# An encoder layer in float32: the output norm's reciprocal roots brought to all partitions by DMA in place of matmuls, and made two steps earlier

## The chip, the cores and the metric

The kernel runs on one core of one Trainium2 chip. The metric is the device time of one execution in microseconds; lower is better. A core has five engines that work side by side, each on its own queue of instructions: PE (TensorE, matmuls; its weight loads are listed as PEld), DVE (VectorE), ACT (ScalarE), POOL (GpSimd) and SP (SyncE, which here issues nearly all DMA transfers). Each engine takes its instructions strictly in order, and an instruction that waits holds up all that stand behind it on the same engine. SBUF is the memory on the core, with 128 partitions; PSUM holds what PE writes, in eight banks; DRAM is reached by DMA.

## The reference

One layer of an encoder, applied with the same weights to a prompt of 2048 tokens and a sample of 512, each with 16 learned meta tokens ahead:

```python
def mixer_layer(h, norm_g, w_in, na_rpb, sink, w_proj_a, w_proj_b, w_out, t5_bias):
    u = rms_norm(h, norm_g)
    proj = u @ w_in                                   # 1024 x 5376
    qa, ka, va, za, qb, kb, vb, zb, ga, gb = jnp.split(proj, cuts, axis=-1)
    o_a = neighbourhood_attention(qa, ka, va, na_rpb) # 8 heads, 8 x 16 window of a 64-wide grid
    o_b = window_attention(qb, kb, vb, t5_bias, sink) # 8 query heads, 2 key heads, +-128 tokens
    y_a = (o_a * silu(za)) @ w_proj_a
    y_b = (o_b * silu(zb)) @ w_proj_b
    merged = sigmoid(ga) * y_a + sigmoid(gb) * y_b
    return merged @ w_out

h = h + mixer_layer(h, ...)
y = rms_norm(h[:, N_META:], final_g)                  # x * rsqrt(mean(x * x) + 1e-6) * g
```

All data is float32. The change touches both norms: the one at the input, for two of the five windows of tokens, and the one at the output, for four of the five.

## The kernel before, in words

Everything is kept with features on the partitions and tokens along the free axis. The 2560 tokens are five windows of 512: window 0 is the sample, 1 to 4 are the prompt. A float32 product is made of three matmuls of a high and a low part (`mm3`); the low part of a weight tile is a subtraction, on DVE or, in the later stages, on POOL (`wt`, line 190).

*The input projection* comes first, in two passes over the weights, each for two windows (`pairs`, with the products of line 762), and stages in which window 4 is projected alone. `prep_ahead(2)` runs as a generator between the products of the first pass. It sums the squares of windows 2 and 3 on POOL, sums them over the partitions with 8 matmuls against a column of ones (`fin_v`, line 468), makes the reciprocal roots on DVE (`rsqrt`, lines 142 to 152, three Newton steps), and so holds them as a 128 x 8 tile: token c * 128 + p on partition p, column c. What it needs is a row with all 512 values on every partition. For that `diagonal` (line 166, DVE) puts each column on the diagonal of a 128 x 128 block, `spread` (line 174, PE) multiplies the blocks with ones into a PSUM bank, and ACT copies the bank to SBUF (`rsa`, line 486). DVE then scales the inputs by it (line 359).

*Attention and the dense stages* follow. The loop at the end of the program takes attention units of 128 queries, and between them pulls steps from a generator `dense` of the window before: `dense_pb`, `dense_out` (the projection `w_out`), and `dense_pa` of the window itself. A step is half an output tile of `dense_pa` (six matmuls) and the like. `dense_out` leaves its result in `hT` (8 tiles), and POOL adds the squares to `ssq` (line 1245). `dense_fin(w - 1)` is the output norm: four matmuls sum `ssq` over the partitions (`sums`, line 159), then `rsqrt`, `diagonal`, five steps later `spread` and ACT's copy to `rbs` (line 1255), and then in each step POOL multiplies one `hT` by `rbs` (line 1259) and SP stores it (`out_dram`). `with_fill` interleaves it with `dense_pa`: after each step of `dense_pa` one of `dense_fin`. It runs four times, for windows 0 to 3; window 4's norm is made elsewhere (`finish_end`) and is not touched.

PSUM in this part: two banks `s` for scores, three `tp` for transpositions of the softmax, one `o`, and two `d` for the dense products. In the first part: five `mm` and three `vt`.

The order on PE is the order of the program's text. The orders on DVE, ACT, POOL and SP are made by a scheduler from the text and a model of times. A DMA that SP issues waits on SP for what it reads and for the buffer it fills. DMAs use eight completion counters in turn, and one also waits for the DMA that had its counter before. SP's line is 131 (`move`) for all.

Of the kernel before, what the change touches and what calls it, by code (L numbers as in the profile page):

```python
# [9 lines left out]
F32 = mybir.dt.float32  # L10
# [7 lines left out]
P = 128  # L18
# [7 lines left out]
WTOK = 512  # L26
NWIN = TOK // WTOK
# [60 lines left out]
def encoder_block(ctx: ExitStack, tc: tile.TileContext, xT, x_end, w_in, w_pa, w_pb, w_o, norm_g, final_g,  # L88
                  final_row, bias_a0, bias_a1, bias_a2, bias_a3, bias_b, bias_b0, outT_p, outT_s, out_e):
    nc = tc.nc  # L90
# [4 lines left out]
    def dt(name, shape):  # L95
        return dram.tile(shape, F32, tag=name, name=name)
# [9 lines left out]
    vb_d = dt("vb", [TOK, 2, P])  # L106
    vbm_d = dt("vbm", [N_META, 2, P])
    z_d = {(b, w, p): dt(f"z{b}{w}{p}", [P, WTOK]) for b in "ab" for w in range(NWIN) for p in range(4)}
    pre_d = dt("pre", [P, 4, 7, WTOK])
    wo_d = [dt(f"wo{c}", [P, 2, KT, WTOK]) for c in range(2)]  # L110
    g_d = {(b, w, f): dt(f"g{b}{w}{f}", [P, WTOK]) for b in "ab" for w in range(NWIN) for f in range(KT)}
# [27 lines left out]
    def rsqrt(small, sq, m, nc_):  # L139

        ve, hv, r, t = (small.tile([P, 8], F32, tag=f"rs{i}", name=f"rs{i}")[:m, :nc_] for i in range(4))
        nc.vector.tensor_scalar(ve, sq, 1.0 / D_MODEL, EPS, ALU.mult, ALU.add)
        nc.vector.tensor_scalar(r.bitcast(I32), ve.bitcast(I32), 1, None, ALU.arith_shift_right)
        nc.vector.tensor_scalar(r.bitcast(I32), r.bitcast(I32), -1.0, float(0x5F3759DF), ALU.mult, ALU.add)
        nc.vector.tensor_scalar(hv, ve, -0.5, None, ALU.mult)
        for _ in range(3):
            if nc_ == 1:
                nc.vector.scalar_tensor_tensor(t, r, hv, r, ALU.mult, ALU.mult)
            else:
                nc.vector.tensor_mul(t, r, hv)  # L150
                nc.vector.tensor_mul(t, t, r)
            nc.vector.scalar_tensor_tensor(r, t, 1.5, r, ALU.add, ALU.mult)
        return r
# [9 lines left out]
    def diagonal(dg, r, m):  # L163

        nc_ = r.shape[1]
        nc.vector.tensor_mul(dg[:m, : nc_ * m].rearrange("p (c n) -> p c n", n=m),
                             ident[:m, None, :m].broadcast_to([m, nc_, m]),
                             r[:m, :, None].broadcast_to([m, nc_, m]))

    def spread(psum, tag, dg, m, nc_):  # L170

        rb = psum.tile([P, WTOK], F32, tag=tag, name="rs_rb")
        for c in range(nc_):
            nc.tensor.matmul(rb[:, c * P : c * P + m], ones[:m, :], dg[:m, c * m : c * m + m], start=True, stop=True)
        return rb

    wpool = ctx.enter_context(tc.tile_pool(name="wpool", bufs=2))
    lo_eng, low = [nc.vector], [None]
# [269 lines left out]
    def prep_ahead(w):  # L448


        x0 = st.tile([P, 4, WTOK], F32, tag="x0", name="xa", bufs=1)
        x = x0[:, 2:4]
        for n in range(KT):
            k, i = n // 2 * 2, n % 2
            move(x, xT[k * P : (k + 2) * P, (w + i) * WTOK : (w + i + 1) * WTOK].rearrange("(k p) t -> p k t", p=P))
            yield
            acc = x0[:, i]
            nc.scalar.activation(x, x, AF.Square)
            if n < 2:
                nc.gpsimd.tensor_add(acc, x[:, 0, :], x[:, 1, :])  # L460
            else:
                for j in range(2):
                    nc.gpsimd.tensor_add(acc, acc, x[:, j, :])
            yield
        v = ps_t.tile([P, WTOK], F32, tag="vt", name="fin_v")
        for i in range(2):
            for c in range(4):
                nc.tensor.matmul(v[:, 4 * i + c : 4 * i + c + 1], x0[:, i, c * P : (c + 1) * P], ones[:, 0:1],
                                 start=True, stop=True)
        r = rsqrt(uxp, v[:, :8], P, 8)  # L470
        dgs = [ev.tile([P, WTOK], F32, tag="t", name="rs_dg", bufs=3) for _ in range(2)]
        for i in range(2):
            diagonal(dgs[i], r[:, 4 * i : 4 * i + 4], P)
        yield
        for kk in range(4):
            x0 = st.tile([P, 4, WTOK], F32, tag="x0", name="xa", bufs=1)
            for half in range(2):
                move(x0[:, 2 * half : 2 * half + 2],
                     xT[(kk + 4 * half) * P : (kk + 4 * half + 1) * P, w * WTOK : (w + 2) * WTOK]
                     .rearrange("p (i t) -> p i t", t=WTOK))  # L480
            yield
            if kk == 0:
                rss = []
                for i in range(2):
                    rss.append(ev.tile([P, WTOK], F32, tag="t", name=f"rsa{i}", bufs=3))
                    nc.scalar.copy(rss[i], spread(ps_t, "vt", dgs[i], P, 4))
            x = [x0[:, j] for j in range(4)]
            tt = ev.tile([P, 2, WTOK], F32, tag="ev", name="tt")
            for j in range(4):
                scale(x[j], kk, j, rss)  # L490
            nc.vector.tensor_sub(tt[:, 0], x[b22], x[b12])
            nc.vector.tensor_sub(x[b12], x[b12], x[b11])
            nc.vector.tensor_sub(tt[:, 1], x[b22], x[b12])
            t4 = ev.tile([P, 2, WTOK], F32, tag="ev", name="t4")[:, 0]
            nc.vector.tensor_sub(t4, x[b21], tt[:, 1])
            yield
            move(pre_d[:, kk, 0:4], x0)
            move(pre_d[:, kk, 4:6], tt)
            move(pre_d[:, kk, 6], t4)
            yield  # L500
# [669 lines left out]
    pools = {}  # L1170
# [74 lines left out]
                nc.gpsimd.tensor_add(ssq, ssq, x)  # L1245

    def dense_fin(w):
        r = rsqrt(pools["d"], sums(acc["s", w], 0, P, 4, ps_d, "d"), P, 4)
        dg = pools["d"].tile([P, WTOK], F32, tag="rbs", name="rs_dg", bufs=1)
        diagonal(dg, r, P)  # L1250
        for _ in range(5):
            yield
        rb = spread(ps_d, "d", dg, P, 4)
        rbs = pools["d"].tile([P, WTOK], F32, tag="rbs", name="rbs", bufs=1)
        nc.scalar.copy(rbs, rb)
        for f in range(KT):
            hT = acc["h", w, f]
            with tc.issue_after(low[0]):
                nc.gpsimd.tensor_mul(hT, hT, rbs)
            dst = outT_s if w == 0 else outT_p  # L1260
            c0 = 0 if w == 0 else (w - 1) * WTOK
            move(dst[f * P : (f + 1) * P, c0 : c0 + WTOK], hT)
            yield
# [92 lines left out]
    def phases(w, br):  # L1356

        if br == "a":
            if w == 0:
                yield from islice(gates, GATES_A)  # L1360
            else:
                yield from dense_pb(w - 1)
                yield from dense_out(w - 1, range(0, 4))
        elif w == 0:
            yield from gates
            open_dense()
            yield from dense_pa(0)
        else:
            yield from dense_out(w - 1, range(4, 8))
            pa = dense_pa(w)  # L1370
            yield from islice(pa, 3)
            yield from with_fill(pa, dense_fin(w - 1))


# [190 lines left out]
```

## Time and profile before

| what | value |
|---|---|
| median of 3 runs | 1909.06 us (1908.71 to 1910.85) |
| the profiled execution's own time | 1908.84 us |
| its span, first to last instruction | 1906.5 us |
| TensorE clock granted | 0.998 of full speed |
| matmuls `rs_rb` (line 174) in the span | 74 records, first at 31.8 us, last at 1821.6 us |
| multiplications of `hT` on POOL (line 1259) | 32, from 1317.3 us to 1833.6 us |
| DMA | 423.78 MB, q1 busy 66.8% of 16 engines' span |

Times in the profile are microseconds from the span's start. A row of a timeline is: start, length, engine, line, operation, what it writes and reads, shape, count; in brackets the idle time just ahead and what ended it. A row of the waits is: engine, line, what was waited for, total, times, longest. A row of the windows is: the stretch, then busy time and number of instructions of PE, PEld, DVE, ACT and POOL, the granted clock, the DMA share and GB/s. A float32 matmul leaves two records. The span holds four stretches that matter here, one for each `dense_fin`, which begin at about 1299, 1470, 1641 and 1809 us, and one of the first pass, at about 296 to 330 us.

### The profile page before, as it was taken

How to read it: one execution, taken by the hardware profiler on the slowest of the kernel's cores; microseconds unless marked ns; L12 is line 12 of the kernel's file. 1: busy time of each engine (PE TensorE's matmuls, PEld its weight loads, DVE VectorE, ACT ScalarE, POOL GpSimd, SP SyncE). 2: the span in 40 equal slices, each digit the busy share in tenths (PEclk: the TensorE clock that was granted, in tenths of full speed). 3: DMA queues.
4: the chain of work that ended last, by engine and by line, in shares of the span. 5: the costliest groups of instructions: out<-in, count | busy, mean ns of one | idle time of the engine just before them, and what ended most of it. 6: DMA issues, size and time to landing. Idle time of an engine off the chain costs nothing.

```text
span 1906.5 us, 29720 instructions
## 1 busy us (share of the span) xinstructions
PE 1878.5 (99%) x9925; PEld 1599.4 (84%) x9925; DVE 1320.3 (69%) x2887; ACT 1147.6 (60%) x2515; POOL 731.9 (38%) x556
## 2 busy tenths in 40 slices
PE   8999999999999999999999999999999999999998
PEld 6998888888888888888878888888888888888886
DVE  8886455556477544445457788878987887888874
ACT  6454443434464444444356787797788788878932
POOL 2005342323103232323223335655844773585420
PEclk9999999999999999999999999999999999999999
DMA  7667554645296765644368877977986996697473
GB/s 261 218 190 293 175 198 165 218 174 177 83 353 218 239 210 194 194 138 160 105 207 289 254 217 261 294 223 242 319 270 185 307 316 217 197 326 252 124 289 141
DMA packets 223760, 423.78 MB, mean 222 GB/s; under 512 B 49640, under 2 KB 90808, under 8 KB 222072
## 3 DMA queue, kind: packets, MB, share of 16 engines
q1 hardware_dynamic: 223320, 421.88, 66.8%
q8 instruction: 79, 1.29, 0.3%
q14 instruction: 73, 0.60, 0.1%
q10 hardware_dynamic: 288, 0.01, 0.0%
HBM read 303.07 MB, written 118.74 MB: 221 GB/s over the span
## 4 chain that ended last, share of the span: by engine, by line
PE 75%; DVE 9%; ACT 6%; DMA 5%; issue 3%; POOL 2%; SPq 0%; ACTq 0%; DVEq 0%; POOLq 0%
PE pa L762 21%; PE pe L762 10%; PE pc L762 5%; PE mm L135 4%; PE mm L137 4%; PE mm L136 4%; PE tp L1027 2%; PE pso L137 2%; PE pso L135 2%; PE pso L136 2%; PE tp L1129 1%; PE oa L1044 1%; PE oa L1042 1%; DVE s L953 1%; DMA wo<-wos 1%
## 5 line engine op out<-in xcount | busy, mean ns | idle before, releaser
L190 POOL TENSOR_TENSOR wt<-wraw,wt 128x512 fp32r<-128x512 f32 x164 | 215.4, 1331 | 288.2 <-ACT wt L189 288.1
L762 PE MATMUL pa<-u,wt 128*128 128x512 f32 x1008 | 242.9, 390 | 0.0
L762 PE MATMUL pa<-u,x 128*128 128x512 f32 x984 | 237.8, 390 | 0.0
L189 ACT CAST wt<-wraw 128x512 fp32r<-128x512 f32 x312 | 177.9, 620 | 73.8 <-PE mm L137 37.6
L762 PEld LDWEIGHTS pa<-u,wt 128*128 128x128 f32 x1008 | 188.7, 188 | 39.0
L762 PEld LDWEIGHTS pa<-u,x 128*128 128x128 f32 x984 | 183.9, 188 | 38.1
L733 POOL TENSOR_TENSOR s<-wraw,raw 128x512 f32<-128x512 f32 x40 | 57.9, 1447 | 271.7 <-DVE x L190 271.7
L135 PE MATMUL mm<-u,wt 128*128 128x512 f32 (+2 forms) x416 | 151.6, 364 | 7.3 <-ACT u L316 7.3
L728 POOL TENSOR_TENSOR s<-raw 128x512 f32<-128x512 f32 x40 | 60.0, 1500 | 253.3 <-DMA raw<-in_w_in_dram 137.0
L136 PE MATMUL mm<-u,wt 128*128 128x512 f32 (+2 forms) x416 | 147.5, 355 | 1.5 <-DVE u L317 1.5
L137 PE MATMUL mm<-u,wt 128*128 128x512 f32 (+2 forms) x416 | 147.5, 355 | 0.8 <-DVE wt L190 0.8
L190 DVE TENSOR_TENSOR wt<-wraw,wt 128x512 fp32r<-128x512 f32 x148 | 104.6, 746 | 61.6 <-ACT wt L189 61.5
L762 PE MATMUL pe<-u,wt 128*128 128x512 f32 x504 | 121.9, 391 | 0.0
L762 PE MATMUL pc<-u,wt 128*128 128x512 f32 x504 | 121.1, 389 | 0.0
L1031 DVE TENSOR_TENSOR pl<-tp,ph 128x512 fp32r<-128x512 f32 (+7 forms) x160 | 98.8, 617 | 24.0 <-ACT ph L1030 22.3
L762 PE MATMUL pe<-u,x 128*128 128x512 f32 x480 | 115.3, 389 | 0.0
L960 ACT ACTIVATE pr<-s,nm 128x384 f32<-128x384 f32 (+5 forms) x160 | 91.3, 571 | 37.9 <-DVE nm L953 35.4
L762 PEld LDWEIGHTS pc<-u,wt 128*128 128x128 f32 x504 | 94.6, 188 | 19.6
L762 PEld LDWEIGHTS pe<-u,wt 128*128 128x128 f32 x504 | 94.2, 188 | 19.4
L741 POOL TENSOR_TENSOR s<-wraw,s 128x512 f32<-128x512 f32 x40 | 52.9, 1322 | 146.2 <-DVE wt L190 146.2
L1030 ACT CAST ph<-tp 128x512 fp32r<-128x512 f32 (+7 forms) x160 | 84.7, 529 | 38.7 <-PE tp L1027 36.5
L135 PE MATMUL pso<-mh,wt 128*128 128x512 f32 x256 | 107.1, 418 | 0.0
(238 smaller groups left out, 5050.7 us busy)
## 6 DMA issues: line engine op xcount, KB each, us to landing
wraw<-in_w_in_dram SPq DMA_DIRECT2D x86, 512.0 KB
qa<-evq SPq DMA_DIRECT2D x20, 1024.0 KB
raw<-in_w_in_dram SPq DMA_DIRECT2D x40, 512.0 KB
q<-qa SPq DMA_DIRECT2D x20, 1024.0 KB
wraw<-in_w_o_dram SPq DMA_DIRECT2D x32, 512.0 KB
kbt<-kb SPq DMA_DIRECT2D x32, 384.0 KB
qb<-evq SPq DMA_DIRECT2D x20, 512.0 KB
ka<-evk SPq DMA_DIRECT2D x20, 512.0 KB
```

What stands on the lines that cost most here:

```text
L135: nc.tensor.matmul(ps, wh, uh, start=first, stop=False)
L136: nc.tensor.matmul(ps, wh, ul, start=False, stop=False)
L137: nc.tensor.matmul(ps, wl, uh, start=False, stop=last)
L189: nc.scalar.copy(h, r)
L190: low[0] = (eng or lo_eng[0]).tensor_sub(l, r, f32(h)).ins
L728: eng.tensor_add(s1, a21, a22)
L733: eng.tensor_sub(s3, a11, a21)
L741: eng.tensor_sub(s4, a12, s2)
L762: nc.tensor.matmul(ps, wt[:, a, s], u[:, b, kk, :], start=first and kk == 0 and i == 0, stop=kk == 3 and i == 2, skip_group_check=True)
L960: nc.scalar.activation(out, s, AF.Exp, bias=nm, scale=-1.0, accum_out=sm)
L1030: nc.scalar.copy(ph_[:kb, a], tb)
L1031: nc.vector.tensor_sub(pl_[:kb, a], tb, f32(ph_[:kb, a]))
```

## The change

`spread`, `diagonal` and ACT's copies are gone from `dense_fin` and `prep_ahead`. In their place the 128 x 4 (128 x 8) tile of reciprocal roots is stored to a small DRAM tensor in the order of tokens (`r_d`, `rp_d`), and loaded back with every partition reading the same 2 KB. The two other users of `spread`, early in the program, stay. In `dense_fin` the sums take a `tp` bank instead of a `d` bank, and it begins after one step of `dense_pa` in place of three.

```diff
+    r_d = {w: dt(f"r{w}", [4, P]) for w in range(NWIN - 1)}
+    rp_d = dt("rp", [8, P])
...
+    def in_all(r):
+
+        return r.rearrange("c p -> (c p)")[None, :].broadcast_to([P, WTOK])
...   (prep_ahead)
-        r = rsqrt(uxp, v[:, :8], P, 8)
-        dgs = [ev.tile([P, WTOK], F32, tag="t", name="rs_dg", bufs=3) for _ in range(2)]
-        for i in range(2):
-            diagonal(dgs[i], r[:, 4 * i : 4 * i + 4], P)
+        move(rp_d.rearrange("c p -> p c"), rsqrt(uxp, v[:, :8], P, 8))
         yield
...
+            if kk == 0:
+                rss = [ev.tile([P, WTOK], F32, tag="t", name=f"rsa{i}", bufs=3) for i in range(2)]
+                for i in range(2):
+                    move(rss[i], in_all(rp_d[4 * i : 4 * i + 4]))
             yield
-            if kk == 0:
-                rss = []
-                for i in range(2):
-                    rss.append(ev.tile([P, WTOK], F32, tag="t", name=f"rsa{i}", bufs=3))
-                    nc.scalar.copy(rss[i], spread(ps_t, "vt", dgs[i], P, 4))
...
     def dense_fin(w):
-        r = rsqrt(pools["d"], sums(acc["s", w], 0, P, 4, ps_d, "d"), P, 4)
-        dg = pools["d"].tile([P, WTOK], F32, tag="rbs", name="rs_dg", bufs=1)
-        diagonal(dg, r, P)
-        for _ in range(5):
-            yield
-        rb = spread(ps_d, "d", dg, P, 4)
+        r = rsqrt(pools["d"], sums(acc["s", w], 0, P, 4, ps_p, "tp"), P, 4)
+        move(r_d[w].rearrange("c p -> p c"), r)
+        yield
+        yield
         rbs = pools["d"].tile([P, WTOK], F32, tag="rbs", name="rbs", bufs=1)
-        nc.scalar.copy(rbs, rb)
+        move(rbs, in_all(r_d[w]))
+        yield
+        yield
         for f in range(KT):
...   (phases)
             pa = dense_pa(w)
-            yield from islice(pa, 3)
+            yield from islice(pa, 1)
             yield from with_fill(pa, dense_fin(w - 1))
```

What this does to the order of instructions is seen at three places, all in the first `dense_fin`; the other windows are alike.

SP, around the loads of the gates `sga` for `dense_pa`, before:

```order
L131 DMA sga<-ga_172 128x512
L131 DMA wraw<-in_w_pb_dram 128x2x512
L131 DMA kd<-ka_97 128x960
L131 DMA kd<-kam_101 128x64
L131 DMA q<-qa_66 128x2x1024
L131 DMA ba<-in_bias_a_dram 128x1280
L131 DMA sga<-ga_173 128x512
L131 DMA sga<-ga_174 128x512
L131 DMA wraw<-in_w_pb_dram 128x2x512
L131 DMA sga<-ga_175 128x512
L131 DMA out_dram<-hT 128x512 x4
```

and now (lines are two higher):

```order
L133 DMA sga<-ga_177 128x512
L133 DMA r_157<-rs_12801 128x4x1
L133 DMA rbs<-r_157 128x512
L133 DMA wraw<-in_w_pb_dram 128x2x512
L133 DMA kd<-ka_97 128x960
L133 DMA kd<-kam_101 128x64
L133 DMA q<-qa_66 128x2x1024
L133 DMA ba<-in_bias_a_dram 128x1280
L133 DMA sga<-ga_178 128x512
L133 DMA out_dram<-hT 128x512 x3
L133 DMA sga<-ga_179 128x512
L133 DMA wraw<-in_w_pb_dram 128x2x512
```

The store `r` and the load `rbs` stand between the third `sga` and the next weight tile, and the first three stores of `hT` now stand ahead of the second weight tile.

POOL, from the last square sum on, before (`wt` are weight splits, `y` and `yb` the attention output times its gate and its low part):

```order
L1245 TENSOR_TENSOR ssq<-ssq,xres 128x512
L190 TENSOR_TENSOR wt<-wraw,wt 128x512 x4
L1259 TENSOR_TENSOR hT<-hT,rbs 128x512 x4
L1166 TENSOR_TENSOR y_12412<-y_12412,z 128x512
L190 TENSOR_TENSOR wt<-wraw,wt 128x512 x2
L1259 TENSOR_TENSOR hT<-hT,rbs 128x512 x4
L978 TENSOR_TENSOR yb_12549<-y_12412,yb_12548 128x512
L1166 TENSOR_TENSOR y_12487<-y_12487,z 128x512
L190 TENSOR_TENSOR wt<-wraw,wt 128x512 x2
L978 TENSOR_TENSOR yb_12549<-y_12487,yb_12548 128x512
```

and now:

```order
L1247 TENSOR_TENSOR ssq<-ssq,xres 128x512
L196 TENSOR_TENSOR wt<-wraw,wt 128x512 x2
L1261 TENSOR_TENSOR hT<-hT,rbs 128x512 x3
L196 TENSOR_TENSOR wt<-wraw,wt 128x512 x2
L1261 TENSOR_TENSOR hT<-hT,rbs 128x512 x4
L1168 TENSOR_TENSOR y_12404<-y_12404,z 128x512
L196 TENSOR_TENSOR wt<-wraw,wt 128x512 x2
L1261 TENSOR_TENSOR hT<-hT,rbs 128x512
L980 TENSOR_TENSOR yb_12541<-y_12404,yb_12540 128x512
L1168 TENSOR_TENSOR y_12479<-y_12479,z 128x512
L980 TENSOR_TENSOR yb_12541<-y_12479,yb_12540 128x512
L196 TENSOR_TENSOR wt<-wraw,wt 128x512 x2
```

Three `hT` stand ahead of the second pair of weight splits, and the second `yb` ahead of the last pair.

PE, where the spread stood before:

```order
L1158 MATMUL ob<-pl,vb 64x256
L1015 MATMUL s<-kd,q 128x512
L1016 MATMUL s<-kd,q 128x512
L174 MATMUL rs_rb<-rs_dg,ones 128x128 x4
L135 MATMUL psa<-ya_11125,wt 128x512
```

and now:

```order
L1158 MATMUL ob<-pms_8434,vms 64x128 x2
L1160 MATMUL ob<-pl,vb 64x256
L1017 MATMUL s<-kd,q 128x512
L1018 MATMUL s<-kd,q 128x512
L137 MATMUL psa<-ya_11117,wt 128x512
```

The four matmuls of the spread are gone. The four matmuls of the sums stand ahead of the third half-step of `dense_pa`, where they stood ahead of the fifth.

## The prediction

> **What bounds the kernel now.** I read the busy table of the page first, then the waits of the matmul engine and of its weight loader, then the timeline around each place where the reciprocal roots are made, and last the windows between them.
>
> ```profile
> PE 1878.5 (99%) x9925; PEld 1599.4 (84%) x9925; DVE 1320.3 (69%) x2887; ACT 1147.6 (60%) x2515; POOL 731.9 (38%) x556
> ...
> PE psb L136 <- POOL yb L978: 2.9, 3, 1.3
> PE psa L135 <- ACT rbs L1255: 2.6, 3, 0.9
> ...
> PEld tp L1027 <- DVE pr L971: 4.9, 10, 0.8
> PEld psb L136 <- POOL yb L978: 4.2, 3, 1.8
> PEld psa L135 <- ACT rbs L1255: 3.5, 3, 1.2
> ...
> 1466.00:1486.00 20.00, 20.00 (x127) 17.76 (x126) 18.29 (x55) 14.14 (x40) 5.21 (x4) 1.00 0.68 235
> ```
>
> PE is busy 99% of the span, so the program is a chain of matmuls, and an instruction taken off PE shortens it by the step from its start to the next start, unless another engine is close behind. The lower rows are waits (total, times, longest): PE and its loader wait three times for ACT's copy of the spread row, and three times for POOL's `yb`. The last row is one of the stages concerned: PE 20.00 of 20 us, DVE 18.29, ACT 14.14, POOL 5.21. PE paces it, with DVE 9% behind.
>
> **What comes off PE.** The timeline of the first of the four `dense_fin`, PE and ACT rows (start, length):
>
> ```profile
> 1313.13 1.05 PE L174 MATMUL rs_rb<-rs_dg,ones 128*128 128x128 f32 x8
> 1313.94 0.48 PE L135 MATMUL psa<-ya,wt 128*128 128x512 f32 x1
> ...
> 1316.07 0.27 PE L1132 MATMUL tp<-ident,prs 128*32 128x128 f32 x1
> 1316.64 0.57 ACT L1255 COPY rbs<-rs_rb 128x512 f32<-128x512 f32 x1
> 1317.27 0.50 PE L135 MATMUL psa<-ya,wt 128*128 128x512 f32 x1 [0.93 <-ACT rbs L1255]
> ...
> 317.98 1.95 PE L174 MATMUL rs_rb<-rs_dg,ones 128*128 128x128 f32 x16
> 319.68 2.99 PE L762 MATMUL pa<-u,wt 128*128 128x512 f32 x12
> ```
>
> The spread of four matmuls (eight records) holds PE from 1313.13 to 1313.94, 0.81 us; four of them make 3.24 us. The spread took one of the two `ps_d` banks, so the next `psa` waits until ACT has copied it out: from 1316.07 to 1317.27, 1.2 us, where a `psa` elsewhere follows a transposition at once. The loader's total for three places is 3.5 us, the matmuls' own 2.6 us; I take 3.5, since start to start is what PE loses, and keep 2.6 as the other end. In the first pass eight matmuls go, 317.98 to 319.68, 1.70 us. The two ACT copies there, DVE's diagonals and ACT's four copies go too; they lie beside PE and I count nothing for them.
>
> **What the earlier sums cost.** The sums' own matmuls stay. They move from ahead of the fifth half-step of `dense_pa` to ahead of the third. There they meet POOL's last addition to `ssq`. For each window, POOL's addition and the PE instruction ahead of which the sums now stand:
>
> ```profile
> 1293.62 1.28 POOL L1245 TENSOR_TENSOR ssq<-ssq,xres 128x512 f32<-128x512 f32 x1
> 1294.50 0.48 PE L135 MATMUL psa<-ya,wt 128*128 128x512 f32 x1
> ...
> 1464.08 1.28 POOL L1245 TENSOR_TENSOR ssq<-ssq,xres 128x512 f32<-128x512 f32 x1
> 1465.06 0.48 PE L135 MATMUL psa<-ya,wt 128*128 128x512 f32 x1
> ...
> 1634.96 1.29 POOL L1245 TENSOR_TENSOR ssq<-ssq,xres 128x512 f32<-128x512 f32 x1
> 1635.95 0.48 PE L135 MATMUL psa<-ya,wt 128*128 128x512 f32 x1
> ...
> 1803.58 1.28 POOL L1245 TENSOR_TENSOR ssq<-ssq,xres 128x512 f32<-128x512 f32 x1
> 1804.64 0.48 PE L135 MATMUL psa<-ya,wt 128*128 128x512 f32 x1
> ```
>
> The additions end at 1294.90, 1465.36, 1636.25 and 1804.86; PE arrives 0.40, 0.30, 0.30 and 0.22 us before that. With about 0.05 us from POOL's end to PE's start (the `yb` rows below) this is a new wait of 1.4 us in all. Its ends: nothing, if POOL gets there sooner, and one POOL operation more in each place, 4 x 1.28 = 5.1 us. Behind the waiting sums stand all of PE's matmuls, so it is paid in full.
>
> **What the new place of POOL's work is worth.** POOL multiplies `hT` by the row. Before, eight of these stand late, and the last `yb` behind them comes late for PE:
>
> ```profile
> 1332.72 1.28 POOL L1166 TENSOR_TENSOR y<-y,z 128x512 f32<-128x512 f32 x1
> 1334.49 2.73 POOL L190 TENSOR_TENSOR wt<-wraw,wt 128x512 fp32r<-128x512 f32 x2 [0.49 <-ACT wt L189]
> 1337.17 1.29 POOL L978 TENSOR_TENSOR yb<-y,yb 128x512 fp32r<-128x512 f32 x1
> ...
> 1337.31 0.39 PE L135 MATMUL psb<-yb,wt 128*128 128x512 f32 x1
> 1338.51 0.50 PE L136 MATMUL psb<-yb,wt 128*128 128x512 f32 x1 [0.81 <-POOL yb L978]
> ```
>
> In the new order the second `yb` stands ahead of that `wt` pair (2.73 us), and three `hT` more are done by then. If POOL starts on `hT` some 8 us sooner (next part), this wait goes. Its ends are 0 and the loader's 4.2 us; I take the middle, 2.1, because the new `yb` also needs ACT to cast `y` earlier than it does now.
>
> **What the way through DRAM costs.** DVE's Newton steps come first, then SP issues the store of the row, waits for it to land, and issues the load:
>
> ```profile
> 1301.16 0.16 DVE L142 TENSOR_SCALAR rs<-fin_v 128x4 f32<-128x4 f32 x1
> 1302.52 1.22 DVE L144 TENSOR_SCALAR rs<-rs 128x4 int32<-128x4 int32 x1
> 1308.20 0.14 DVE L152 SCALAR_TENSOR_TENSOR rs<-rs,rs 128x4 f32<-128x4 f32 x1
> 1301.17 2.54 POOL L190 TENSOR_TENSOR wt<-wraw,wt 128x512 fp32r<-128x512 f32 x2 [6.28 <-ACT wt L189]
> ...
> 1294.92 5.89 SPq L131 DMA_DIRECT2D sga<-ga  x3
> 1303.74 0.38 SPq L131 DMA_DIRECT2D wraw<-in_w_pb_dram  x1
> ...
> 0.74 0.40 SPq L131 DMA_DIRECT2D wraw<-in_w_in_dram  x1
> 4.46 1.14 ACT L189 CAST wt<-wraw 128x512 fp32r<-128x512 f32 x2 [1.79 <-DMA wraw<-in_w_in_dram]
> 1902.83 0.81 SPq L131 DMA_DIRECT2D out_dram<-h  x2
> ```
>
> From the first of these DVE steps to the last are 7.2 us. Started 4.7 us sooner they end at about 1302 to 1303. SP has then issued its third `sga` (1294.92 + 5.89 = 1300.8) and before the change stands idle until 1303.74, so its wait for DVE costs nothing; only the wait for the row's landing holds up `wraw`, `kd`, `q` and `ba` behind it. The trace has no store of 4-byte pieces. Nearest rows: the last output store lands within 2.9 us of its issue (1903.64 to the span's end at 1906.5), and a load of 512 KB on idle queues takes 3.7 us (0.74 to 4.46). Store and load then take 5.8 to 7.4 us, and the row is there at about 1309, against 1317.3 for the first `hT` before. `wraw` issues some 3 us later than at 1303.74, and its cast is at 1311.49, so I count nothing for that. If that cover is gone, ACT's cast, POOL's split and then PE are late by as much.
>
> In the first pass the row's load stands behind the two `xa` loads, whose consumers wait for them now:
>
> ```profile
> 324.62 3.83 DVE L359 SCALAR_TENSOR_TENSOR xa<-xa,ng,rsa 128x512 f32<-128x512 f32 x4 [4.44 <-DMA xa<-in_xT_dram]
> ```
>
> Two loads of 256 KB more delay DVE here by 1 to 2 us, after 4.44 us in which it idled; PE does not wait for DVE in that stage, so it is hidden.
>
> **The transposition bank.** The sums leave `ps_d` and take one of three `tp` banks, so the next unit's transpositions take a bank one turn younger. A wait there is bounded by nothing and by the longest that the loader shows for a transposition, 0.8 us, four times 3.2 us. I take 1.0 us in all.
>
> **The sum**, against the profiled execution's own 1908.84 us: -3.24 - 3.5 - 1.70 - 2.1 + 1.4 + 1.0 = -8.1 us, 1900.7 us. The median shown, 1909.06, is 0.2 us above that execution, which gives 1900.9 us. The best ends (-3.24 - 3.5 - 1.70 - 4.2) give -12.6, or 1896.4; the worst of all terms together (-3.24 - 2.6 - 1.70 + 5.1 + 3.2) give +0.8, or 1909.9.
>
> **Rivals.** A change under 0.2%, 3.8 us, is about what a measurement of this kernel cannot tell from none.
>
> *The late row (slower).* POOL now has three `hT` ahead of a `wt` pair:
>
> ```profile
> 1312.18 2.66 POOL L190 TENSOR_TENSOR wt<-wraw,wt 128x512 fp32r<-128x512 f32 x2 [8.47 <-ACT wt L189]
> ...
> 1323.32 0.48 PE L135 MATMUL psa<-ya,wt 128*128 128x512 f32 x1
> ```
>
> That pair feeds the `psa` of 1323.32, which PE would now reach at about 1321.8 (less 0.81 and 1.2, plus 0.45). Three `hT` of 1.28 us and the pair take 6.5 us, so the row must be there by about 1315.3, 13 us after its store is issued. Beyond that each microsecond costs one in three windows (in the fourth POOL has no `wt`). To lose the 8.1 us and 3.8 more takes 4 us in each, a round trip of 17 us: 1913 us. For it: each store is 512 pieces of 4 bytes (1024 in the first pass), which no row here prices, and SP stands still meanwhile. Against: the 5.8 to 7.4 us above. Chance 0.10.
>
> The Trainium skill ("DMA: Bandwidth & Descriptors", Rules for kernel authors) speaks against this change: a last dimension that is not contiguous becomes one descriptor per element, and it puts a 19-fold difference on transposing by a plain DMA's access pattern. Held against the 2.9 us store, that factor would be an estimate of 55 us, far beyond this rival's 13. The same page (Anatomy of one DMA) gives about 2 us of fixed time per transfer, by which both transfers together would land in an estimated 4 us. No row here shows either.
>
> *DVE paces (no change).* With DVE at 18.29 of 20 us, what PE sheds may return as waits for DVE's scores and splits, leaving the first pass's 1.7 us and little of the rest: about 1906.5. Against: DVE sheds a diagonal too, and its integer steps (1.22 us beside a busy POOL) fall where POOL idles. Chance 0.11.
>
> *The sums wait long (no change).* If POOL's last addition slips by one operation in each window, 5.1 us in place of 1.4: 1904.6, and with the `yb` wait unchanged 1906.7. For it: that addition stands behind a `wt` pair. Chance 0.09.
>
> **How the numbers follow.** The forecast has 0.70, the two quiet rivals 0.20, the late row 0.10. Of the forecast's 0.70 nearly all lies below 1905.2, and a little of the quiet cases too: faster 0.71, same 0.19, slower 0.10. Range 1896.9 to 1907.2: from the best ends to beyond the quiet rivals, leaving out the late row and the far ends of both sides. It is nearly the forecast's own range.
>
> **What would show it.** In the new profile no `rs_rb` after the first 60 us; the `psa` wait for ACT's copy gone; four waits of PE on POOL's `ssq`, 0.2 to 0.5 us each; `hT` starting on POOL about 14 us after the sums; the `psb` wait on `yb` smaller. Wrong would be: `hT` waiting more than 13 us from the store, PE waiting on `wt` in these stages, transpositions waiting for a `tp` bank, or PE's new waits on DVE adding up to what was shed.

## The result, and the profile after

The changed kernel takes 1935.78 us (median; 1930.52 to 1942.0) against 1909.06 us: a ratio of 1.0137 with a 95% interval of 1.0123 to 1.0150. It is slower by 1.4%, where 1900.9 us was forecast and the range ended at 1907.2. The profiled execution took 1930.52 us, the shortest of the five, with a span of 1928.7 us; the traces below so show 22.2 us of a loss of 26.7.

First the busy row of the page of the changed kernel, then its waits (total, times, longest), the rows that answer to those shown of before. The new line numbers are 2 higher in the dense part, 6 higher around the weight splits.

```profile
PE 1884.3 (98%) x9877; PEld 1598.8 (83%) x9877; DVE 1307.4 (68%) x2881; ACT 1142.2 (59%) x2509; POOL 726.9 (38%) x556
...
POOL hT L1261 <- DMA rbs<-r: 60.8, 4, 22.0
ACT yb L979 <- POOL y L1168: 26.5, 4, 9.2
DVE ta L1205 <- DMA sga<-ga: 21.5, 6, 5.8
...
PE tp L1029 <- DVE pr L973: 8.0, 8, 3.5
PE oa L1044 <- ACT ph L1032: 6.6, 2, 5.3
PE psb L139 <- DVE wt L196: 4.0, 2, 3.3
...
PEld fin_v L161 <- POOL ssq L1247: 1.6, 4, 0.5
```

The waits that were to go are gone: no `psa` waits for ACT's copy, no `psb` for POOL's `yb`. In their place PE waits for DVE's `pr` and `wt` and for ACT's `ph`, and one step further back stand a DMA (`sga`, `rbs`) and POOL. The prediction's own sign of being wrong, "`hT` waiting more than 13 us from the store", is there: 14.5 us in the first place, as the next rows show. PE does 48 instructions less, yet is busy 5.8 us longer; both are taken up below.

Then the timeline of the first of the four places, rows of SP, POOL, DVE and PE (start, length, idle time before it and what ended that):

```profile
1302.91 0.37 SPq L133 DMA_DIRECT2D r<-rs  x1
1311.74 0.32 SPq L133 DMA_DIRECT2D rbs<-r  x1
1312.15 0.40 SPq L133 DMA_DIRECT2D wraw<-in_w_pb_dram  x1
1315.78 0.46 SPq L133 DMA_DIRECT2D sga<-ga  x1
...
1317.37 3.78 POOL L1261 TENSOR_TENSOR hT<-hT,rbs 128x512 f32<-128x512 f32 x3 [14.51 <-DMA rbs<-r]
...
1324.85 0.69 DVE L1205 TENSOR_TENSOR ta<-psa,sga 128x512 f32<-128x512 f32 x1 [5.40 <-DMA sga<-ga]
...
1322.43 0.50 PE L139 MATMUL psa<-ya,wt 128*128 128x512 f32 x1 [0.89 <-POOL wt L196]
1326.41 0.82 PE L1029 MATMUL tp<-ident,pr 128*128 128x128 f32 x4 [2.44 <-DVE pr L973]
1328.31 0.63 PE L137 MATMUL psa<-ya,wt 128*128 128x512 f32 x1
1331.76 0.42 PE L1044 MATMUL oa<-ph,v 128*128 128x256 f32 x2 [1.96 <-DVE y L1165]
```

The store of the row is issued at 1302.91 us, the load only at 1311.74, and the first multiplication starts at 1317.37: 14.5 us for the way through DRAM, 8.8 of them for 2 KB on the way out. `wraw` leaves SP at 1312.15 instead of 1303.74 us.

Last, what the DMA engines did meanwhile: two windows of 4 us and one of 70, before (the first three rows) and after (the next three); the last two columns are the busy share of the DMA engines and the GB/s they moved.

```profile
1304.00:1308.00 4.00, 4.00 (x27) 3.49 (x26) 3.83 (x18) 2.22 (x8) 0.00 (x0) 1.00 0.71 263
1308.00:1312.00 4.00, 4.00 (x24) 3.42 (x23) 3.87 (x15) 3.37 (x10) 0.00 (x0) 1.00 1.03 378
...
1330.00:1400.00 70.00, 68.58 (x405) 58.04 (x404) 61.60 (x144) 55.48 (x121) 52.50 (x42) 1.00 1.01 324
```

```profile
1304.00:1308.00 4.00, 4.00 (x27) 3.56 (x27) 3.87 (x13) 3.22 (x10) 0.00 (x0) 1.00 0.07 4
1308.00:1312.00 4.00, 4.00 (x26) 3.42 (x25) 2.98 (x11) 3.29 (x9) 0.00 (x0) 1.00 0.00 0
...
1330.00:1400.00 70.00, 67.40 (x388) 57.20 (x389) 62.20 (x144) 53.84 (x120) 51.80 (x40) 0.97 1.01 324
```

While the row is on its way, the core's DMA engines move 4 and then 0 GB/s where they moved 263 and 378. And from 1330 to 1400 us they are full in both kernels (share 1.01, the same 324 GB/s): what is not carried before 1330 is carried late. `sga`, issued at 1315.78, is what DVE's `ta` at 1324.85 waited for.

The DMA packets of the changed kernel from 1302.9 to 1305 us, and then from 1305 to 1311.6 us:

```profile
DMA packets 528, 0.00 MB, mean 1 GB/s; under 512 B 528, under 2 KB 528, under 8 KB 528
DMA packets 1, 0.02 MB, mean 2 GB/s; under 512 B 0, under 2 KB 0, under 8 KB 0
```

The small packets, the 512 pieces among them, all start within the first stretch; in the 6.6 us after it the engines carry one packet, and only then is the store taken as landed. What the landing waits for is in no record here.

Where the 22.2 us between the spans arose is read from the same DVE instructions in both traces: the start after less the start before, as the median over a stretch of 20 us. Each column stands for the stretch from that time on; the last column is close to the end. A row is one execution against one: e1 ends 2.3 us late although its median is that of before, so 2 us in the last columns say little.

| kernel (run) | 280 | 460 | 1240 | 1400 | 1600 | 1740 | 1880 |
|---|---|---|---|---|---|---|---|
| the change | -1.69 | -3.51 | -0.83 | +5.60 | +10.75 | +16.39 | +22.20 |
| e1 first pass alone | +0.14 | -1.68 | +0.76 | +0.71 | +0.33 | +2.17 | +2.27 |
| e2 multiplications later | +0.11 | -1.72 | -0.02 | +4.81 | +8.02 | +9.15 | +12.71 |
| e3 pieces of 16 bytes | +0.51 | -1.31 | +1.55 | +2.58 | +0.78 | -2.45 | -3.13 |
| e4 same place, row by PE | -1.67 | -3.49 | +0.26 | +0.60 | -1.10 | -3.46 | -4.17 |
| f1 as e4, dead trip | -1.43 | -3.25 | -1.29 | +9.00 | +13.77 | +16.81 | +17.27 |
| f2 load on POOL's queue | -1.66 | -3.49 | -1.13 | +9.52 | +19.52 | +25.98 | +31.45 |
| f4 place and bank alone | +0.00 | +0.00 | -0.49 | +0.32 | -1.46 | -3.86 | -4.64 |
| g3 both on POOL's queue | +0.25 | -1.57 | +1.07 | +11.20 | +16.57 | +18.50 | +22.58 |
| g4 as e4, dead store | +0.36 | -1.47 | -0.28 | +5.57 | +9.40 | +9.89 | +9.12 |

The first column lies ahead of any changed instruction: a kernel may start 1.7 us apart there. Between 1240 and the end the four places add 6.4, 5.2, 5.6 and 5.8 us.

### The profile page after: what moved, and what is told of

Same layout as the page of the kernel before. It is cut to its first block, busy times and chain, and to the rows that moved or that the text cites. A ratio compares the mean times of both kernels' runs of the same rounds, so it can differ in the third digit from the quotient of the medians.

```text
span 1928.7 us, 29626 instructions
## 1 busy us (share of the span) xinstructions
PE 1884.3 (98%) x9877; PEld 1598.8 (83%) x9877; DVE 1307.4 (68%) x2881; ACT 1142.2 (59%) x2509; POOL 726.9 (38%) x556
## 3 DMA queue, kind: packets, MB, share of 16 engines
q8 instruction: 79, 1.29, 0.3%
## 4 chain that ended last, share of the span: by engine, by line
PE 71%; DVE 8%; ACT 7%; DMA 5%; issue 5%; POOL 4%; SPq 0%; POOLq 0%; ACTq 0%; DVEq 0%
PE pa L764 21%; PE pe L764 10%; PE pc L764 5%; PE mm L139 3%; PE mm L138 3%; PE mm L137 3%; PE tp L1029 2%; PE pso L139 2%; PE pso L137 2%; PE pso L138 2%; POOL hT L1261 1%; DMA wo<-wos 1%; PE oa L1046 1%; PE oa L1044 1%; ACT wt L195 1%
## 5 line engine op out<-in xcount | busy, mean ns | idle before, releaser
L743 POOL TENSOR_TENSOR s<-wraw,s 128x512 f32<-128x512 f32 x40 | 53.2, 1330 | 145.2 <-DVE wt L196 145.2
L764 PEld LDWEIGHTS pe<-u,x 128*128 128x128 f32 x480 | 90.1, 188 | 18.7
```

Of the source, the lines that this page charges most:

```text
L743: eng.tensor_sub(s4, a12, s2)
L764: nc.tensor.matmul(ps, wt[:, a, s], u[:, b, kk, :], start=first and kk == 0 and i == 0, stop=kk == 3 and i == 2, skip_group_check=True)
```

## The experiments

**Which part, and is it the place or the row?** Theory L: the row comes too late for the new, earlier place of the multiplications. Rivals: SP standing still until the store has landed (S); the new place itself (P); the first pass.

*e1, the first pass alone.* The four dense places as before, the first pass as in the change:

```diff
     def dense_fin(w):
-        r = rsqrt(..., sums(..., ps_p, "tp"), P, 4)
-        move(r_d[w].rearrange("c p -> p c"), r)
+        r = rsqrt(..., sums(..., ps_d, "d"), P, 4)
+        ...            # diagonal, five steps, spread, copy as before
...
-            yield from islice(pa, 1)
+            yield from islice(pa, 3)
```

> Only the first pass goes through DRAM; the four dense_fin, their place and the bank are as before. In the changed kernel PE was 1.82 us ahead of before at 340 us (offset -1.69 us ahead of the place, -3.51 us behind it), and 0.8 us ahead of it at 1290 us. Theory (all of the loss lies in the dense places): between 1907.0 and 1908.5 us, no wait of PE on the row. Rival (the first pass loses by its 1024 pieces of 4 bytes on SP's queue): above 1912 us.

Measured: 1909.92 us against 1910.16 us, ratio 0.9997 (0.9988 to 1.0005): no difference seen, though a gain of 1.8 us still lies inside the interval; it is 1.4 us above the theory's band and 2 us below the rival's. At its place the first pass gains what was predicted (+0.14 to -1.68, 1.82 us), and in this execution all of it is back by 1240 us.

*e2, the multiplications later.*

```diff
         move(rbs, in_all(r_d[w]))
-        yield
-        yield
+        for _ in range(5):
+            yield
```

> As the change, but five steps instead of two between the row's load and the multiplications, so that these stand where they stood before; the store and the load keep their place. Theory (the row comes too late for the new place of the multiplications): POOL's wait for the row and PE's waits on pr, oa and wt in the three places go, 1900 to 1906 us. Rival (SP's standing still for some 9 us between store and load makes wraw, kd, q and ba late, wherever the multiplications are): SP stands just as long, and the time stays above 1920 us. Second rival (the new place of the multiplications costs by itself, early row or late): 1900 to 1906 us too; the runs e3 and e4 tell that one apart.

Measured: 1928.18 us, ratio 1.0094 (1.0080 to 1.0109). Some 8 us less than the change, but 22 to 28 us above what L asked for, and in S's band. The rows, SP, POOL and DVE:

```profile
1303.73 0.37 SPq L133 DMA_DIRECT2D r<-rs  x1
1312.69 0.32 SPq L133 DMA_DIRECT2D rbs<-r  x1
...
1318.38 5.04 POOL L1261 TENSOR_TENSOR hT<-hT,rbs 128x512 f32<-128x512 f32 x4 [4.00 <-DMA rbs<-r]
...
1326.14 0.69 DVE L1205 TENSOR_TENSOR ta<-psa,sga 128x512 f32<-128x512 f32 x1 [5.50 <-DMA sga<-ga]
```

With the multiplications back in their old place, `ta` waits 5.50 us for `sga` all the same. L alone falls.

*e3, the same order, other pieces.*

```diff
-        move(r_d[w].rearrange("c p -> p c"), r)
+        move(r_d[w].rearrange("c p -> (c p)").rearrange("(p c) -> p c", c=4), r)
```

> As the change, every instruction in the same order, but the four dense rows are stored as 128 pieces of 16 bytes instead of 512 of 4 (the row then holds the same numbers in another order, so the outputs are scaled by the wrong tokens' roots; the amount of work is the same). If the store's 8.8 us from issue to the load's issue come from its pieces, it lands in 3 to 4 us, the row is there some 5 us sooner (hT at 1312 instead of 1317.4), and by the theory of the late row most of the loss goes: 1902 to 1914 us. If the pieces don't matter: 1930 to 1940 us as the change. Rival (the place itself costs): the row comes sooner, yet the time stays above 1925 us.

Measured: 1905.57 us, ratio 0.9984 (0.9973 to 0.9994), 30 us below the change with every instruction in the same order. SP, POOL, and the DMA window (last columns):

```profile
1305.30 0.32 SPq L133 DMA_DIRECT2D r<-rs  x1
1307.32 0.32 SPq L133 DMA_DIRECT2D rbs<-r  x1
...
1312.06 3.92 POOL L1261 TENSOR_TENSOR hT<-hT,rbs 128x512 f32<-128x512 f32 x3 [6.80 <-DMA rbs<-r]
...
1312.00:1316.00 4.00, 4.00 (x26) 3.48 (x25) 3.49 (x8) 2.68 (x7) 3.94 (x4) 1.00 1.05 411
```

The same 2 KB in 128 pieces takes 2.0 us from issue to issue instead of 8.8 (2.0 to 3.2 in the four places). The loss is in the pieces; whether in their number or in their 4 bytes isn't told apart, since both change here.

*e4, the same place, the row by PE.*

```diff
         r = rsqrt(pools["d"], sums(acc["s", w], 0, P, 4, ps_p, "tp"), P, 4)
-        move(r_d[w].rearrange("c p -> p c"), r)
-        ...
+        dg = pools["d"].tile([P, WTOK], F32, tag="rbs", name="rs_dg", bufs=1)
+        diagonal(dg, r, P)
+        for _ in range(4):
+            yield
+        rb = spread(ps_d, "d", dg, P, 4)
+        rbs = pools["d"].tile([P, WTOK], F32, tag="rbs", name="rbs", bufs=1)
+        nc.scalar.copy(rbs, rb)
```

> As the change in the first pass, in the bank of the sums and in the place of everything, but the row of each dense window is spread by PE and copied by ACT as before, four steps behind the sums. POOL's order is that of the change, SP's too but for the row's store and load. The spread can run at about 1309, so the row is there at about 1311, some 6 us sooner than in the change. Theory of the late row: 1902 to 1910 us (the spread's 3.2 us and ACT's copy are back). Rival (the place of the multiplications ahead of wt and y costs by itself, or the sums in the tp bank): above 1922 us.

Measured: 1904.20 us, ratio 0.9968 (0.9956 to 0.9980), faster than the kernel before. POOL:

```profile
1310.30 3.78 POOL L1260 TENSOR_TENSOR hT<-hT,rbs 128x512 f32<-128x512 f32 x3 [6.35 <-ACT rbs L1256]
```

P falls: in the new place, with the row there at 1310.3 us, the dense part gains 4.4 us (+0.26 to -4.17).

**SP's standing still, or the pieces themselves?**

*f1, e4 with the trip as dead weight.*

```diff
         diagonal(dg, r, P)
-        for _ in range(4):
-            yield
+        move(r_d[w].rearrange("c p -> p c"), r)
+        yield
+        yield
+        dead = pools["d"].tile([P, P], F32, tag="dead", name="dead", bufs=1)
+        move(dead, r_d[w][0:1].broadcast_to([P, P]))
+        yield
+        yield
```

> e4 (row by PE, 1904.2 us) with the DRAM trip added back as dead weight: the same store of 512 pieces of 4 bytes in the same place of SP's queue and, behind it, a load of 128 numbers of it into a tile that nobody reads. The row itself is there early, by PE. So this prices SP's standing still alone. From e2, where the multiplications were late and SP stood about 9 us in each window all the same and the dense part lost 12.7 us: theory now (SP's standing still delays sga, wraw, kd, q behind it, and this is most of the loss): 1912 to 1922 us, with DVE's ta waiting 3 to 5 us for sga in each of three windows. Rival (only the late row at POOL costs): 1903 to 1906 us.

Measured: 1928.9 us, ratio 1.0092 (1.0072 to 1.0111): 25 us more than e4 by a trip whose data nobody uses, 7 us more than the upper end expected. SP and POOL:

```profile
1311.35 0.32 SPq L133 DMA_DIRECT2D dead<-r  x1
...
1308.75 3.78 POOL L1266 TENSOR_TENSOR hT<-hT,rbs 128x512 f32<-128x512 f32 x3 [6.35 <-ACT rbs L1262]
```

The row is there at 1308.75 us. A late row isn't needed for most of the loss.

*f2, the load on POOL's queue.*

```diff
-        move(rbs, in_all(r_d[w]))
+        nc.gpsimd.dma_start(rbs, in_all(r_d[w]))
```

> As the change, but the row's load in the four dense places is issued on POOL's queue, so that SP issues wraw, kd, q, ba and sga at once behind the store; the store's 512 pieces, and so the late row (POOL's multiplications at about 1317 us), stay. This prices the late row alone. Theory that SP's standing still is most of the loss: 1906 to 1916 us. Rival (the late row alone costs it, through the output stores that wait on SP for hT ahead of sga, and through y and wt on POOL): 1922 to 1936 us.

Measured: 1939.51 us, ratio 1.0153 (1.0135 to 1.0171). That is above even the rival's band, and the trace says why. SP issues `wraw` and the rest at once behind the store, POOL waits for the store, and the window shows what the DMA engines did:

```profile
1302.61 0.37 SPq L133 DMA_DIRECT2D r<-rs  x1
1303.07 0.46 SPq L133 DMA_DIRECT2D wraw<-in_w_pb_dram  x1
...
1312.76 0.71 POOL L1255 DMA_DIRECT2D rbs<-r  x1 [10.20 <-DMA r<-rs]
...
1308.00:1312.00 4.00, 4.00 (x27) 3.49 (x26) 2.98 (x10) 3.38 (x9) 0.00 (x0) 1.00 0.23 31
```

Over 2 MB of loads stand issued, and 31 GB/s are moved. SP did not wait for the landing (only the issue of `sga`, its sixth load, took long, 3.62 us), and the loads hardly ran. The row's load from POOL's queue is slower too: 8.2 us to the first `hT` at 1320.91, where the change has 5.6. So this run doesn't price the late row alone, as it was meant to; it shows that S as I put it isn't the whole: without SP's wait the transfers behind the store are held up as well.

*f3, the row in token order.* A form whose outputs keep their order, with the store of e3 (16-byte pieces) and this change in the sums:

```diff
-            nc.tensor.matmul(v[:m, c : c + 1], ssq[:, c0 + c * m : c0 + (c + 1) * m], ones[:, 0:1],
+            nc.tensor.matmul(v[:m, c : c + 1], ssq[:, c0 + c : c0 + c + (m - 1) * nc_ + 1 : nc_], ones[:, 0:1],
```

> As the change, but the sums take every fourth token for one column (weights with a stride of four), so that the rsqrt tile holds four neighbouring tokens in each partition: its store is 128 pieces of 16 bytes and the row is in the right order, the outputs are the reference's. Each matmul of the sums reads its weights with that stride; if that costs PE nothing, as e3: 1903 to 1908 us. If the strided weights load slower: up to 1 us more in each window.

Measured: 1912.52 us, ratio 1.0011 (1.0000 to 1.0023), at the upper edge of what was allowed for slower weights. The sums, first in e3, then in f3:

```profile
1296.49 1.05 PE L161 MATMUL fin_v<-ones,ssq 128*128 128x1 f32 x8 [0.20 <-POOL ssq L1247]
```

```profile
1295.74 2.03 PE L161 MATMUL fin_v<-ones,ssq 128*128 128x1 f32 x8 [0.20 <-POOL ssq L1247]
```

With a stride in the weights they take 1.0 us longer, 4 us in four places. The rest against e3, 3 us (1 us by the ratios), is not explained.

*f4, place and bank alone*, nothing through DRAM (the diff is against the kernel before):

```diff
-        r = rsqrt(pools["d"], sums(acc["s", w], 0, P, 4, ps_d, "d"), P, 4)
+        r = rsqrt(pools["d"], sums(acc["s", w], 0, P, 4, ps_p, "tp"), P, 4)
-        for _ in range(5):
+        for _ in range(4):
-            yield from islice(pa, 3)
+            yield from islice(pa, 1)
```

> The kernel before with only the two steps sooner, four steps instead of five ahead of the spread, and the sums in the tp bank; no row goes through DRAM, in the first pass neither. If the first pass's change is worth nothing in the end (e1: 1909.92 against 1910.16 us), the time is that of e4: 1903 to 1906 us. If it is worth its 1.8 us: 1905 to 1908 us.

Measured: 1905.51 us, ratio 0.9979 (0.9968 to 0.9990), as e4 within the intervals, and a few lines without DRAM are faster than before. The time lies in both bands expected, so whether the first pass's 1.8 us survive to the end is not settled: e4, which has them, is 1.3 us lower (2.1 by the ratios), less than the intervals can tell.

**Does another queue help, and what does the store do by itself?**

*g3, store and load on POOL's queue.*

```diff
-        move(r_d[w].rearrange("c p -> p c"), r)
+        nc.gpsimd.dma_start(r_d[w].rearrange("c p -> p c"), r)
-        move(rbs, in_all(r_d[w]))
+        nc.gpsimd.dma_start(rbs, in_all(r_d[w]))
```

> As the change, but the four dense rows' stores (512 pieces of 4 bytes) and loads are both issued on POOL's queue, so that nothing of SP's queue stands behind the pieces. In f2, where SP's loads stood behind the store without SP waiting, the core moved only 31 GB/s from 1308 to 1312 us. Theory Q (the pieces hold up the queue they are in): SP's loads run from about 1303 us, sga comes in time, only the late row on POOL is left: 1906 to 1920 us, with over 200 GB/s in that stretch. Theory E (the pieces hold up the DMA engines, whatever the queue): as f2, 1930 to 1942 us, with under 100 GB/s.

Measured: 1935.12 us, ratio 1.0133 (1.0115 to 1.0151), as theory E had it. POOL issues the store, SP its loads from 1305.23 us on:

```profile
1304.02 0.92 POOL L1251 DMA_DIRECT2D r<-rs  x1 [0.52 <-DVE rd L966]
...
1306.29 0.38 SPq L133 DMA_DIRECT2D wraw<-in_w_pb_dram  x1
...
1308.00:1312.00 4.00, 4.00 (x28) 3.56 (x27) 3.32 (x10) 3.00 (x9) 0.00 (x0) 1.00 0.81 31
1312.00:1316.00 4.00, 4.00 (x24) 3.34 (x23) 2.92 (x9) 2.55 (x7) 0.57 (x1) 1.00 0.44 26
```

31 and 26 GB/s, though the pieces now are in another queue than the loads. (POOL's load takes longer here as well, 8.6 us to the first `hT`.) The Trainium skill ("DMA: Bandwidth & Descriptors", Issuing engines are not separate DMA queues) says that all issuing engines' transfers run on the same 16 DMA engines and interleave; this trace, with these two numbers, fits the first half, and shows how little came through beside the pieces. Where the transfers are held it doesn't show: the share of the DMA engines was 0.81 and 0.44 here, but 0.23 in f2 and 0.29 in g4.

*g4, e4 with only the dead store.* f1 without the `dead` tile and its load.

> f1 (row by PE, 1928.9 us) without the dead load: only the store of 512 pieces of 4 bytes is left in SP's queue in each window, and no instruction of SP waits for it. Theory (the pieces themselves hold up the transfers behind them for some 9 us, whether SP waits or not): 1915 to 1930 us, and under 100 GB/s from 1304 to 1311 us. Rival (f1's loss comes from SP waiting for the landing before it issues wraw, kd, q, ba, sga): 1903 to 1908 us, and over 200 GB/s there.

Measured: 1917.79 us, ratio 1.0034 (1.0021 to 1.0047), within the theory's band and above the rival's.

```profile
1303.46 0.37 SPq L133 DMA_DIRECT2D r<-rs  x1
1303.92 0.46 SPq L133 DMA_DIRECT2D wraw<-in_w_pb_dram  x1
...
1308.00:1312.00 4.00, 3.70 (x21) 3.27 (x22) 2.76 (x9) 2.73 (x8) 2.24 (x2) 1.00 0.29 31
1312.00:1316.00 4.00, 4.00 (x27) 3.50 (x26) 3.42 (x7) 2.47 (x7) 4.00 (x4) 1.00 0.43 47
```

No instruction waits for this store's landing (but for the DMA that has its counter next, an `out_dram` issued 12 us later), and PE makes the row in time (`hT` at 1309.76 us); four stores of 2 KB cost 13.6 us against e4 (1917.8 - 1904.2; by the ratios 0.66% of 1910, 12.6 us). SP is held all the same, by the issue of `sga`, 5.36 us long. Waiting for the landing on SP, with the load behind it, makes f1's 11 us more, and the change, whose row is late besides, lies another 6.9 us above f1 (8.6 by the ratios): 13.6, 11.1 and 6.9 us make up the 31.6 us between e4 and the change.

*g1, 16-byte pieces read back in order.* e3, with POOL's read of the row in strides, so that each token meets its own root:

```diff
-                nc.gpsimd.tensor_mul(hT, hT, rbs)
+                h3 = hT.rearrange("q (c p) -> q c p", c=4)
+                nc.gpsimd.tensor_mul(h3, h3, rbs.rearrange("q (p c) -> q c p", c=4))
```

> As e3 (128 pieces of 16 bytes), and the outputs are now the reference's: POOL's multiplication reads the row with a stride of four numbers, so that each token meets its own root; the sums keep their plain weights, which cost 1.02 to 1.05 us in e3 against 2.00 to 2.03 us with f3's stride. If POOL reads with the stride at 1.28 us as before: as e3, 1903 to 1908 us. If a strided read takes POOL longer, its hT pass 1.5 us each and wt and y behind them come late: 1908 to 1915 us.

Measured: 1917.26 us, ratio 1.0037 (1.0023 to 1.0050), above both bands. POOL's eighth `hT` and DVE's longest instruction:

```profile
1328.09 1.53 POOL L1262 TENSOR_TENSOR hT<-hT,rbs 128x512 f32<-128x512 f32 x1
...
1321.70 9.42 DVE L973 TENSOR_SCALAR pr<-pr,rd 128x512 f32<-128x512 f32 x1
...
1331.18 1.11 PE L1029 MATMUL tp<-ident,pr 128*128 128x128 f32 x4 [6.95 <-DVE pr L973]
```

The strided read takes 1.53 us instead of 1.28, as the second expectation had it. But in the profiled execution, the slowest of the eleven (1923.24 us), the largest wait comes from one `pr` on DVE, 9.42 us long where 0.7 is common: it begins within an unbroken run of POOL (1318.39 to 1330.84 us) and ends 0.3 us behind that run. A second one, in the next window, took 8.71 us. No other run has a `pr` over 1.62 us behind 1250 us, nor has e3 with nearly the same run of POOL; why it struck here, and whether it does in the faster executions, is open.

*g2, the bank alone.* The kernel before with `ps_p, "tp"` for `ps_d, "d"` in the sums, nothing else.

> The kernel before with nothing but the sums in the tp bank; place and spread as before. f4 (bank and two steps sooner) took 0.21% off. If the bank is worth nothing by itself: 1908.5 to 1910.5 us, and f4's gain is that of the place. If the bank is the gain (the sums no longer wait for one of two ps_d banks): 1904 to 1907 us. The prediction's +1.0 us for a later tp bank would make it 1909.5 to 1911 us.

Measured: 1910.96 us, ratio 0.9999 (0.9990 to 1.0007): no difference seen. (The kernel before took 1910.95 us beside it, so the ratio counts here and not the bands in microseconds.) f4's gain is that of the place.

## Why the prediction was wrong, step by step

**The step that failed** is the way through DRAM, "store and load then take 5.8 to 7.4 us". It measured 14.5, 14.8, 15.0 and 15.5 us in the four windows (`r` issued to the first `hT`). The estimate took a big store's landing time, 2.9 us, for a store of 512 pieces of 4 bytes; that store alone took 8.8 to 10.7 us until the load could be issued, and in e3, with 128 pieces, 2.0 to 3.2. With those the whole way took 6.4 to 7.6 us, nearly the 5.8 to 7.4 of the prediction: it had the order of events right and the store's price wrong. The Trainium skill's page that the prediction held against itself ("DMA: Bandwidth & Descriptors", Rules for kernel authors) was right in direction: four times as many pieces, each a quarter as long, took 3.4 to 4.4 times as long. Its 19-fold, which it states for transposing, would have been 55 us, far too much; the 2 us of fixed time (Anatomy of one DMA, a section on transfers that POOL issues) fit e3's store only.

**A second error sat in "so I count nothing for that".** I looked at the wait on SP and asked what is behind it on SP: `wraw`, "some 3 us later". It was 8.4 us, and the right question was what is behind the store on the DMA engines. In g4 nobody waits for the store's landing, and 13 us are lost. As I read it, that is because some 2.5 MB that before were carried from 1304 to 1312 us (4 us at 263 GB/s and 4 at 378) are held until the store has landed, just ahead of 70 us in which the DMA engines are full. The DMA share stood in the windows of before; I read only the issue times.

**The rival of the late row** had the right sign and 0.10. Its mechanism is in the traces: in the change `psa` waits 0.89 us for POOL's `wt` behind a row that came 2.1 us after its limit of 1315.3, and in f2 4.65 us behind one that came 5.6 us after it. It was priced at 1913 us, through POOL alone. What it left out: DVE's `ta` behind a late `sga` (then `pr`, then PE, 2.44 us), ACT's `yb` cast behind POOL's `y` (26.5 us in four places; then `ph` and `ol`, then PE, up to 5.3 us), and the clock. How much the late row would cost by itself, with the DMA engines free, no run shows: every run that made it late also held up the transfers. On top of held transfers it is worth 6.9 us in the change against f1 (less what the missing spread gives back), and 21.7 us in f2, where the row is later still, against g4.

**The clock.** PE's idle time grew by 16.4 us (44.4 against 28.0, span less busy). Its busy time grew by 5.8 us although 4.9 us of spreads were gone, so what is left costs some 10.7 us more. Windows of the changed kernel behind its long waits; the third number from the end is the granted clock:

```profile
1326.00:1338.00 12.00, 8.98 (x33) 6.72 (x34) 7.34 (x17) 4.56 (x12) 10.23 (x9) 0.72 1.00 327
1503.00:1514.00 11.00, 9.49 (x40) 7.28 (x41) 7.54 (x19) 4.97 (x13) 8.83 (x7) 0.69 1.01 297
1683.00:1695.00 12.00, 11.65 (x57) 9.80 (x58) 10.77 (x25) 7.63 (x20) 8.82 (x7) 0.77 0.93 301
1857.00:1866.00 9.00, 8.58 (x27) 6.85 (x28) 5.46 (x10) 2.38 (x4) 0.00 (x0) 0.69 1.01 391
```

Behind pauses of 2.44, 3.47, 5.34 and 3.26 us the granted clock is 0.50, for 3.4 us twice in the first place and for 6.8 us in the other three, and a 128x512 matmul takes 0.63 us instead of 0.39. So to 16.4 us of waits come another 10.7 for the lower clock. The Trainium skill ("TensorE: Matmul & The Clock Gate", Part 1: The HAM clock gate) has an idle window of about 3.4 us after which the clock is halved; here pauses of 2.13 and 2.25 us were enough (e2). The pause's length alone doesn't decide: behind 2.88 us in f1 and 2.40 us in g3 the clock stayed full, and in f3 it fell to 0.50 at 1641.8 us for 3.4 us with no wait of PE over 0.3 us in the 9 us before. The clock is nearly half of the change's own loss but not its origin: f1 lost 0.9% at a mean clock of 0.998, that of before.

**The other terms**, each by the run that shows it:

- The spread (0.81) and the `psa` stall (1.2): PE's offset in the first place falls from -0.42 to -2.53 us before the losses begin, 2.1 us where 2.0 were counted. Right.
- The sums' new wait, +1.4: the loader's row has 1.6 us, 4 times, 0.5 at most. Right.
- The `yb` wait, -2.1: gone entirely in e3 and e4, where the row is in time. Right, and on the small side.
- The bank, +1.0: g2 shows no difference, though 1.0 us lies inside its interval. Without weight.
- The first pass, -1.70: 1.82 us at its place, but no difference seen at the end (e1). In the change's trace part of it comes back as waits of PE for DVE that before did not show: 0.7 us on `tkv` at 657 us, 0.2 on `u` at 984, 0.5 on `pr` at 1214; and in e1, e3 and e4 the pause of 1.49 us near 987 us was followed by a lower clock, while before the clock stayed full behind it. The prediction had "DVE paces" as a rival for the dense places and did not apply it here.
- The sum of what e3 leaves, with the row in time: 1905.57 us by a ratio of 0.9984, 3 us gained where 8.1 were summed. About 1.8 of the rest is the first pass, if e1's trace holds; PE's waits for `pr` in e3 (5.0 us, against 1.4 before) hold most of what is left.

**What would have been the better change**: only the place. e4 and f4 keep PE's spread and move the sums two half-steps sooner: 0.9968 and 0.9979 of the time before.

## What to carry to other kernels

Count a transfer's pieces before its bytes, and ask what it holds up on the DMA engines, not only who waits for it: four stores of 2 KB, in 512 pieces each, cost this kernel 13 us even when nobody read them. Such a transfer seems dearest just ahead of a stretch in which the DMA share is 1.0, since what it delays there isn't made up; the first pass's 1024 pieces, with a share of 0.14 from 324 to 332 us behind them, cost nothing at their place. No run varied that alone. And where PE may wait two microseconds or more, expect a lower clock behind most such waits; where it is 99% busy, a microsecond taken off may come back as a wait for the next engine (e1's trace).

## What was not expected of the hardware

- In the changed kernel 512 pieces of 4 bytes took 8.8 to 10.7 us to land, though in the first place all of them started within 2 us of the issue; 128 pieces of 16 bytes took 2.0 to 3.2 us (e3). In the first place the core's DMA moved 26 to 72 GB/s in windows of 4 us during the former, whichever queue they were in (f2 and g3, from 1304 to 1312 us; in g3 also to 1316), with over 2 MB issued.
- The granted clock fell to 0.50, for 3.4 or 6.8 us, behind all seven pauses of PE of 2.1 us or more in the traces of before, the change and e1 to e4 (from 50 us on), and behind three of seven of 1.5 us there. It is no rule: pauses of 2.88 us (f1) and 2.40 us (g3) were not followed by it, and f3 shows it once without a pause.
- A stride of 16 bytes in fp32 weights made eight records of the sums take 2.03 instead of 1.05 us (f3, e3); the same stride in one operand of POOL's multiplication made it 1.53 us instead of 1.28 (g1).
- One DVE instruction of 0.7 us lasted 9.42 us beside an unbroken run of POOL (g1), another 8.71.
